# Mix-out in two pairs of column blocks, with earlier loads of the memory's and the residual's rows

## The chip, the cores and the metric

The kernel runs on one core of one Trainium2 chip. The metric is the device time of one execution in microseconds (us). Engines: PE (TensorE) multiplies, PEld is its weight load, DVE (VectorE) and ACT (ScalarE) do elementwise work, POOL (GpSimd) a few small operations, SP (SyncE) issues the DMAs. SBUF is the on-chip memory, PSUM the accumulator that PE writes.

## The reference

One decoder layer over 256 tokens of width 2048, all in fp32. In outline:

```python
hn = rmsnorm(h, norm_mix_w)
q, k, v, g_ret, xr, yr, g_a, g_b = split(hn @ w_in)
ret_out = silu(g_ret) * head_groupnorm(retention(q, k, v))
rnn_out = gelu(yr) * rg_lru(causal_conv(xr))
merged = sigmoid(g_a) * (ret_out @ w_proj_ret) + sigmoid(g_b) * (rnn_out @ w_proj_rnn)
h = h + merged @ w_mix_out                       # "mix-out"
h = h + memory_cross_attention(rmsnorm(h), rmsnorm(mem), xa_w_q, xa_w_k, xa_w_v, xa_w_o)
h = h + conv_gated_ffn(rmsnorm(h))
out = rmsnorm(h, final_norm_w)
```

`mem` is 256 fixed memory tokens of width 2048. The change lies between `w_proj_ret` and the first product of the cross-attention, `mem_n @ xa_w_k`.

## The kernel before

Each fp32 operand is split into a high and a low part in the fp32r type, and a product of two operands is three matmuls (high x high, low x high, high x low). Tokens are two tiles of 128 (`tt`), the sum runs over k-tiles of 128 (16 of them for width 2048), and the output columns come in blocks of 512 (`BW`). A matmul here is always 128x128 weights against 512 columns.

Weights are streamed once from one array in the order of use (`weight_plan`, `weight_stream`). `prefetch` loads a chunk of 1 MB into one of three buffers called `raw`; `weight_parts` makes the high part with an ACT cast (`hi`, L351) and the low part with a DVE subtraction (`lo`, L352), into six buffers of each. It runs two chunks ahead of PE (`AHEAD`).

A product with a weight comes in two forms. `steps_n` does one block of 512 columns; a chunk is four k-tiles. `steps_pair` does two blocks together; a chunk is two k-tiles (a "k-pair") of both blocks. Both chunks are 24 matmuls. In a pair, chosen k-pairs (the tuple `seven`) are done in seven block products in place of eight: the two token tiles, the two k-tiles and the two column blocks make a 2x2x2 block product, and sums and differences of blocks are multiplied. That is 21 matmuls. It asks for sums of the weights (`seven_parts`: four DVE additions at L372, and seven half-size parts in place of four) and sums of the left operand (`sums_of`, L450 to L461), kept in a table (`token_sums`) for the next product with the same operand. The result of a pair is put together from its PSUM banks by one ACT copy (L518), four DVE operations (L525) after the last seven-product k-pair, and four more (L536) at its end.

The work of a pair or block is followed by a step that needs it transposed. `by_dma` copies rows into two 16-bit planes (ACT, L558, called planes below), transposes them by a DMA from SP (L559), and some chunks later `join` puts the words together (ACT, L571) and hands them on. `later(n, fn)` runs `fn` when `n + 1` more chunks have been written down. Large tiles share 29 buffers (`big`). A scheduler orders each engine's instructions by their place in the program and by when they could run; the matmuls keep the program's order.

Around the change: the gates `g_a` are two pairs of `w_in` (L999 to L1002), then come two pairs of `w_proj_ret` (L1003 to L1007). Each of their four results is gated, added (L978, L1006) and sent through `by_dma` to `turn_merged`, which makes two left operands of mix-out from each block, eight in all. Then `residual` does mix-out in four single blocks. Its first three blocks are run by halves: the first half of k of blocks 0, 1 and 2, then the second half of each, and then block 3 (`by_halves` puts the weights in that order). Just before it, eight loads of 512 KB are issued: four of the rows of `x` (`hrow`, the residual) and four of the rows of `mem`. During it the squares of `mem` are summed (ACT, L646), the mean is turned into a factor, and the first four transposed and split tiles of `mem` (`ms`) are made (L617 on ACT, L618 on DVE). After each block the residual is added (L1029), the sum goes through `by_dma` to `turn` (split of the next left operand, L617 and L618), and its squares are taken (ACT, L1047). Four rows are parked in HBM. The same `residual` serves `xa_w_o`, with its first two blocks as a pair.

Of the kernel before, what the change touches and what calls it, by code (L numbers as in the profile page):

```python
# [20 lines left out]
NT = D // P  # L21
# [7 lines left out]
BW = 512  # L29
# [14 lines left out]
SEVEN_U = (4,)  # L44
MORE_U = (2, 4)
SEVEN_V = (5,)

O_Q, O_K, O_V, O_G = 0, 1024, 2048, 4096
O_XR, O_YR, O_GA, O_GB = 6144, 8192, 10240, 12288
# [26 lines left out]
def weight_plan():  # L76

    plan = []
    for g in range(2):
        keys = [("w_in", 0, NT, c + g * BW) for c in (O_Q, O_K)]  # L80
        values = [("w_in", 0, NT, O_V + b * BW) for b in range(2)]
        plan += keys + [both("w_in", O_V + 1024, SEVEN_V)] if g else [keys[0], values[0], keys[1], values[1]]
        plan.append(both("w_in", O_G + g * 1024))
    for b in range(4):
        plan += [("w_in", 0, NT, c + b * BW) for c in (O_XR, O_YR)]
    plan += [("w_in", 0, NT, O_GB + b * BW) for b in range(2)] + [both("w_proj_rnn", 0)]
    plan += [both("w_in", O_GB + 1024), both("w_proj_rnn", 1024)]
    plan += [both(w, c + b * BW) for w, c in (("w_in", O_GA), ("w_proj_ret", 0)) for b in (0, 2)]
    plan += [("w_mix_out", 0, NT, b * BW) for b in range(4)]
    plan += [both("xa_w_k", 0, SEVEN_V), both("xa_w_q", 0), both("xa_w_q", 2 * BW), both("xa_w_k", 2 * BW)]  # L90
    plan += [both("xa_w_v", 0)] + [("xa_w_v", 0, NT, b * BW) for b in (2, 3)]
    plan += [both("xa_w_o", 0, SEVEN_O)] + [("xa_w_o", 0, NT, b * BW) for b in (2, 3)]
    for kind, *a in ff_plan():
        if kind == "down" and sum(a) < NF // 4:
            plan += [both("ffn_w_down", b * BW, SEVEN, a[0] * BW, 4 * a[1]) for b in (0, 2)]
        elif kind == "down":
            plan += [("ffn_w_down", a[0] * BW, 4 * a[1], b * BW) for b in range(4)]
        else:
            plan.append(both("ffn_w_up", a[0] * BW, MORE_U if plan[-1][0] != "ffn_w_up" else SEVEN_U, apart=FF))
    return plan  # L100
# [28 lines left out]
    return [c for o in products for c in o[:-1]] + [o[-1] for o in products]  # L129


def by_halves(products):

    return [c for part in (slice(0, 2), slice(2, 4)) for o in products for c in o[part]]


def weight_stream():

    out = [
        [(w, row + k * P, n, (*c[:2], k // KH in c[2]) if isinstance(c, tuple) else c) for k, n in pieces(i, nk, c)]  # L140
        for i, (w, row, nk, c) in enumerate(weight_plan())
    ]
    out[:2] = [[one for pair in zip(*out[:2]) for one in pair]]
    out[-4:-1] = [in_turn(out[-4:-1])]
    i = [c[0][0] for c in out].index("w_mix_out")
    out[i : i + 3] = [by_halves(out[i : i + 3])]
    return [one for chunks in out for one in chunks]


# [17 lines left out]
def hybrid_layer(  # L167
# [47 lines left out]
    def load_rows(src, c, cs=slice(0, BW), t=None):  # L215

        if t is None:
            t = big([P, 2, BW], s="nat")
        rows = src[0].rearrange("(t p) d -> p t d", p=P)
        sp.dma_start(out=t[:, :, cs], in_=rows[:, :, c * BW + cs.start : c * BW + cs.stop])  # L220
        return t
# [34 lines left out]
    plan = weight_plan()  # L256
# [122 lines left out]
    def later(n, fn):  # L379

        pending.append((step[0] + n + 1, fn))
# [156 lines left out]
    def pair(*args):  # L538
        return ended(steps_pair(*args))
# [10 lines left out]
    def by_dma(rows, then, wait=1, pin=False):  # L550


        planes = big([P, 2, 2, BW], U16, s="pl")
        turned_ = big([P, 2, 4, S], U16, s="pt")
        words = rows.bitcast(U16).rearrange("p t (n h) -> p t h n", h=2)
        for tt in range(2):
            with tc.high_priority(FREE):
                act.copy(planes[:, tt], words[:, tt])  # L558
            turning = sp.dma_start_transpose(  # L559
                out=turned_.rearrange("p h f s -> p (h f) s")[:, :, tt * P : (tt + 1) * P],  # L560
                in_=planes[:, tt].rearrange("p h n -> p (h n)"),
            )
            if pin:
                behind.append(turning.ins)

        def join():
            f = big([P, 4, S], s="f")
            halves_ = f.bitcast(U16).rearrange("p f (s h) -> p h f s", h=2)
            for tt in range(2):
                cs = slice(tt * P, (tt + 1) * P)  # L570
# [16 lines left out]
    def split_pair(src, scale=None):  # L587

        t = big([P, 2, BW], F32R, s="s")
        if scale is None:  # L590
            act.copy(t[:, :, 0:S], src)
            dve.tensor_tensor(out=t[:, :, S:BW], in0=src, in1=t[:, :, 0:S].bitcast(F32), op=ALU.subtract)
        else:
            act.mul(t[:, :, 0:S], src, scale)
            dve.scalar_tensor_tensor(
                out=t[:, :, S:BW], in0=src, scalar=scale, in1=t[:, :, 0:S].bitcast(F32),
                op0=ALU.mult, op1=ALU.subtract,
            )
        return t
# [48 lines left out]
    def sums():  # L648
        return sp_.tile([P, 2, 4], F32, tag="ss0", name=nm("ss"))
# [327 lines left out]
    def gated(t, z):  # L977
        dve.scalar_tensor_tensor(out=z, in0=t, scalar=1.0, in1=z, op0=ALU.add, op1=ALU.mult)  # L978

    merged = []  # L980

    def turn_merged(f):
        for pr in range(2):
            merged.append(split_pair(f[:, 2 * pr : 2 * pr + 2, :], 0.5))

    ts, mb = [], []
    for b in range(2):
# [9 lines left out]
            mb.append(z)  # L997
    for h in range(HEADS):
        later(4 + h, lambda h=h: split_head(h))  # L999
    ts = []  # L1000
    for b in (0, 2):
        ts += [tanh_rows(a, a) for a in pair("w_in", 0, xs, NT, O_GA + b * BW, O_GA + (b + 1) * BW)]  # L1002
    for b in (0, 2):  # L1003
        for i, m in enumerate(pair("w_proj_ret", 0, ret, NT, b * BW, (b + 1) * BW)):
            gated(ts[b + i], m)
            dve.tensor_add(m, m, mb[b + i])  # L1006
            by_dma(m, turn_merged, 1 + (b + i == 3))  # L1007


    hrow = [load_rows(x, c) for c in range(4)]  # L1010
    mnat = [load_half(mem, i) for i in range(4)]
    ms = Pairs(mem_t, p_mem, 3)

    def residual(w, st, out, wcol, steps=None):

        ss = sums()
        products = [steps_n(w, 0, st, NT, b * BW) for b in range(4)]
        sources = []
        for b in range(4):
            if steps:  # L1020
                steps(b)
                if b == 0:
                    for one in products[:3]:
                        for _ in range(2):
                            next(one)
            elif b == 0:
                sources += pair(w, 0, st, NT, 0, BW)
            h = hrow[b]
            dve.tensor_add(h, h, sources.pop(0) if sources else ended(products[b]))  # L1029
            by_dma(h, lambda f, b=b: turn(f, b, out, wcol), 1 + (b == 1), b == 3 and steps is None)  # L1030
            if b < 2:
                later(2 + b, lambda h=h, b=b: squares(h, ss, b))
            else:
                squares(h, ss, b)
        return ss

    def turn(f, b, out, wcol):
        for pr in range(2):
            out.append(split_cols(f[:, 2 * pr : 2 * pr + 2, :], lambda j: wcol(4 * b + 2 * pr + j)))
# [6 lines left out]
        junk = tp.tile([P, BW], F32, tag="tmp", name=nm("junk"))  # L1046
        act.activation(junk[:, 0 : y.shape[1]], y, AF.Square, accum_out=o)  # L1047

    rsms = []

    def memory_steps(b):
        if b == 0:
            ss = sums()[:, :, 0:2]
            for c in range(4):
                later(5 + c, lambda c=c: sum_squares(mnat[c], ss, c))
            later(9, lambda: rsms.append(rstd_rows(ss)))
        if b == 2:
            ms.load(2)
            for k2 in range(4):
                later(2 + k2, lambda k2=k2: ms[k2])  # L1060

    h1s, parked = [], []

    def park(h):
# [1 line left out]
        sp.dma_start(out=t, in_=h)  # L1066
        parked.append(t)

    ss1 = residual("w_mix_out", merged, h1s, p_xa, memory_steps)


    for h in hrow:
# [53 lines left out]
    osp = []  # L1126
# [31 lines left out]
        hrow[b] = t  # L1158

    h2s = []  # L1160
    ss2 = residual("xa_w_o", osp, h2s, p_ffn)
    rs2 = rstd_rows(ss2)


# [180 lines left out]
```

## Time and profile before

| | us |
|---|---|
| median of 3 runs | 1983.33 |
| lowest, highest | 1981.59, 1983.79 |
| the profiled execution's own time | 1982.85 |
| its span in the trace | 1980.9 |
| PE busy in the span | 1961.0 |
| DVE busy in the span | 1644.8 |
| ACT busy in the span | 1394.1 |

The profile's page gives the busy time of each engine and lists groups of instructions by line. A view by stretches of time gives the busy time of each engine in each stretch, the granted clock of TensorE, the share of the DMA engines and their rate. A timeline lists instructions in order with their start, their duration, and in brackets the idle time of the engine before them and who ended it. The busy time of PE is modelled: consecutive matmuls overlap in the list, so what a matmul takes is read from the distance between starts. A row "x2" is two matmuls that follow each other.

### The profile page before, as it was taken

The numbers are of one execution on the slowest core, as the hardware profiler recorded it, in microseconds if no ns is written. First come the engines' busy times: TensorE is split into PE (matmuls) and PEld (weight loads), VectorE is DVE, ScalarE is ACT, GpSimd is POOL, SyncE is SP. The second block draws the span as 40 slices with busy tenths as digits, with TensorE's granted clock in tenths as the row PEclk, the third lists the DMA queues.
The fourth block names the chain that finished last, engine by engine and source line by source line (L and its number), as shares of the span: only waits on it lengthen the run. The fifth ranks groups of instructions, "written<-read, shape, count | busy, mean of one in ns | idle before, by whom it ended". The sixth has DMA issues, their size and how long they took to land. (4 is left out here: it accounts for less than half of the span.)

```text
span 1980.9 us, 24128 instructions
## 1 busy us (share of the span) xinstructions
PE 1961.0 (99%) x8798; PEld 1624.5 (82%) x8798; DVE 1644.8 (83%) x2176; ACT 1394.1 (70%) x1714; POOL 31.6 (2%) x25
## 2 busy tenths in 40 slices
PE   9999999999999999999999999999999999999998
PEld 8888888888888888788888888888877888878887
DVE  6887986899898888668888767888889889899786
ACT  6666658989654656697778677787886477774783
POOL 0000001010000000000000000100000000000000
PEclk9999999999999999999999999999999999999999
DMA  8755567665554555897766666577765576665673
GB/s 332 239 213 169 198 245 204 204 223 192 211 211 173 192 212 192 297 308 245 214 222 215 210 216 219 197 230 212 233 203 182 212 232 213 214 201 204 231 252 110
DMA packets 198344, 429.82 MB, mean 217 GB/s; under 512 B 142161, under 2 KB 146769, under 8 KB 153169
## 3 DMA queue, kind: packets, MB, share of 16 engines
q1 hardware_dynamic: 198224, 428.28, 64.5%
q8 instruction: 69, 1.13, 0.2%
q14 instruction: 51, 0.41, 0.1%
HBM read 390.49 MB, written 4.19 MB: 199 GB/s over the span
## 5 line engine op out<-in xcount | busy, mean ns | idle before, releaser
L352 DVE TENSOR_TENSOR lo<-raw,hi 128x1024 fp32r<-128x1024 f32 (+1 forms) x818 | 953.7, 1189 | 249.2 <-ACT hi L351 244.0
L253 PE MATMUL acc<-hi,s 128*128 128x512 f32 (+1 forms) x3632 | 1113.9, 388 | 0.9 <-ACT hi L351 0.8
L351 ACT CAST hi<-raw 128x1024 fp32r<-128x1024 f32 (+1 forms) x818 | 807.8, 1018 | 417.2 <-DMA raw<-in_wall 111.3
L253 PEld LDWEIGHTS acc<-hi,s 128*128 128x128 f32 x3632 | 679.3, 188 | 140.2 <-ACT hi L351 1.5
L253 PE MATMUL acc<-lo,s 128*128 128x512 f32 (+1 forms) x1816 | 704.5, 388 | 3.9 <-DVE lo L352 3.8
L253 PE MATMUL sm<-hi,s 128*128 128x512 f32 x1568 | 482.9, 389 | 0.0
L253 PEld LDWEIGHTS acc<-lo,s 128*128 128x128 f32 x1816 | 341.2, 188 | 76.3 <-DVE lo L352 6.5
L253 PEld LDWEIGHTS sm<-hi,s 128*128 128x128 f32 x1568 | 294.4, 188 | 61.1
L253 PE MATMUL sm<-lo,s 128*128 128x512 f32 x784 | 305.5, 390 | 2.8 <-DVE lo L352 2.7
L571 ACT COPY f<-pt 128x1024 uint16<-128x1024 uint16 x128 | 166.3, 1353 | 14.8 <-DMA pt<-pl 14.6
L253 PEld LDWEIGHTS sm<-lo,s 128*128 128x128 f32 x784 | 147.2, 188 | 34.8 <-DVE lo L352 4.5
L372 DVE TENSOR_TENSOR raw<-raw 128x512 f32<-128x512 f32 x208 | 143.1, 688 | 3.7
L253 PE MATMUL acc<-hi,ts 128*128 128x512 f32 x312 | 96.2, 389 | 0.0
L558 ACT COPY pl<-o 128x1024 uint16<-128x1024 uint16 x68 | 66.7, 1039 | 7.9 <-DVE o L1006 5.2
L253 PEld LDWEIGHTS acc<-hi,ts 128*128 128x128 f32 x312 | 58.5, 188 | 12.2 <-ACT hi L351 0.2
L253 PE MATMUL acc<-lo,ts 128*128 128x512 f32 x156 | 61.5, 394 | 1.7 <-DVE lo L352 1.7
L558 ACT COPY pl<-rows 128x1024 uint16<-128x1024 uint16 x40 | 39.8, 1042 | 21.1 <-DVE rows L584 10.9
L525 DVE TENSOR_TENSOR o<-o,acc 128x512 f32<-128x512 f32 x62 | 42.2, 681 | 0.2
L536 DVE TENSOR_TENSOR o<-o,acc 128x512 f32<-128x512 f32 x62 | 39.6, 680 | 2.9 <-PE acc L253 2.7
L536 DVE TENSOR_TENSOR o<-o,sm 128x512 f32<-128x512 f32 x62 | 40.8, 680 | 0.3
L1172 DVE SCALAR_TENSOR_TENSOR fv<-f,pf,fv 128x255 f32<-128x255 f32 (+1 forms) x88 | 38.7, 479 | 1.7 <-ACT fv L1170 1.5
L525 DVE TENSOR_TENSOR o<-acc,o 128x512 f32<-128x512 f32 x62 | 39.7, 682 | 0.3
(191 smaller groups left out, 1062.6 us busy)
## 6 DMA issues: line engine op xcount, KB each, us to landing
raw<-in_wall SPq DMA_DIRECT2D x352, 1024.0 KB, 4.8
nat<-in_x SPq DMA_DIRECT2D x8, 512.0 KB, 9.1
raw<-in_wall SPq DMA_DIRECT2D x7, 512.0 KB, 6.1
pt<-pl SPq DMA_TRANSPOSE x128, 3.3
nat<-in_mem SPq DMA_DIRECT2D x4, 512.0 KB, 8.7
home<-nat SPq DMA_DIRECT2D x4, 512.0 KB, 6.2
nat<-home SPq DMA_DIRECT2D x4, 512.0 KB, 7.3
xt<-in_x_t SPq DMA_DIRECT2D x3, 512.0 KB, 8.5
```

Source lines behind the costliest of these rows:

```text
L253: tc.keep_in_program_order(pe.matmul(*a, **k))
L351: act.copy(hi[:, cs], src[:, cs])
L352: dve.tensor_tensor(out=lo[:, cs], in0=src[:, cs], in1=hi[:, cs].bitcast(F32), op=ALU.subtract)
L372: dve.tensor_tensor(out=o, in0=a, in1=b, op=ALU.add)
L525: dve.tensor_tensor(out=o, in0=a, in1=b, op=op)
L536: dve.tensor_tensor(out=o, in0=o, in1=banks[a], op=ALU.add)
L558: act.copy(planes[:, tt], words[:, tt])
L571: act.copy(halves_[:, :, :, cs], turned_[:, :, :, cs])
L1172: dve.scalar_tensor_tensor(out=y[:, s:S], in0=z[:, j, 0 : S - s], scalar=pf[:, 2 - s, t : t + 1], in1=y[:, s:S], op0=ALU.mult, op1=ALU.add,)
```

## The change

Mix-out becomes two pairs: blocks 0 and 1 with k-pair 2 in seven products, blocks 2 and 3 with k-pairs 2 and 5. The order by halves is gone. The four loads of `mem` are issued one by one during the pairs of `g_a` (7, 9, 11 and 13 chunks after their start), each with its squares two chunks later. The factor of `mem` and the first two loads of its transposed tiles come four chunks into `w_proj_ret`. The four loads of the residual's rows come one per chunk in the second pair of `w_proj_ret` (after 9 to 12 of its two pairs' 16 chunks). The first four tiles `ms` are made from the join of the third block of `merged` on, two chunks apart. The join waits of mix-out's results become 1, 2, 1, 2 chunks (they were 1, 2, 1, 1). `xa_w_o` keeps its form.

```diff
+SEVEN_M = (2,)
-    plan += [("w_mix_out", 0, NT, b * BW) for b in range(4)]
+    plan += [both("w_mix_out", 0, SEVEN_M), both("w_mix_out", 2 * BW)]
-def by_halves(products):
-    return [c for part in (slice(0, 2), slice(2, 4)) for o in products for c in o[part]]
-    i = [c[0][0] for c in out].index("w_mix_out")
-    out[i : i + 3] = [by_halves(out[i : i + 3])]
...
-    merged = []
+    merged, rsms, hrow = [], [], []
+    ms = Pairs(mem_t, p_mem, 3)
+    ss_mem = sums()[:, :, 0:2]
+    def memory_squares(c):
+        t = load_half(mem, c)
+        later(1, lambda: sum_squares(t, ss_mem, c))
+    def memory_begun():
+        rsms.append(rstd_rows(ss_mem))
+        ms.load(2)
     def turn_merged(f):
         for pr in range(2):
             merged.append(split_pair(f[:, 2 * pr : 2 * pr + 2, :], 0.5))
+            if len(merged) == 5:
+                for k2 in range(4):
+                    later(2 + 2 * k2, lambda k2=k2: ms[k2])
...
+    for c in range(4):
+        later(6 + 2 * c, lambda c=c: memory_squares(c))
     ts = []
     for b in (0, 2):
         ts += [tanh_rows(a, a) for a in pair("w_in", 0, xs, NT, O_GA + b * BW, O_GA + (b + 1) * BW)]
+    later(3, memory_begun)
+    for b in range(4):
+        later(8 + b, lambda b=b: hrow.append(load_rows(x, b)))
...
-    hrow = [load_rows(x, c) for c in range(4)]
-    mnat = [load_half(mem, i) for i in range(4)]
-    ms = Pairs(mem_t, p_mem, 3)
-    def residual(w, st, out, wcol, steps=None):
+    def residual(w, st, out, wcol, paired):
...
         for b in range(4):
-            if steps:
-                steps(b)
-                if b == 0:
-                    for one in products[:3]:
-                        for _ in range(2):
-                            next(one)
-            elif b == 0:
-                sources += pair(w, 0, st, NT, 0, BW)
+            if b in paired:
+                sources += pair(w, 0, st, NT, b * BW, (b + 1) * BW)
             h = hrow[b]
             dve.tensor_add(h, h, sources.pop(0) if sources else ended(products[b]))
-            by_dma(h, lambda f, b=b: turn(f, b, out, wcol), 1 + (b == 1), b == 3 and steps is None)
+            by_dma(h, lambda f, b=b: turn(f, b, out, wcol), 1 + (b % 2 if b in (*paired, *(i + 1 for i in paired)) else 0), b == 3 and w == "xa_w_o")
...
-    def memory_steps(b):
-        if b == 0:
-            ss = sums()[:, :, 0:2]
-            for c in range(4):
-                later(5 + c, lambda c=c: sum_squares(mnat[c], ss, c))
-            later(9, lambda: rsms.append(rstd_rows(ss)))
-        if b == 2:
-            ms.load(2)
-            for k2 in range(4):
-                later(2 + k2, lambda k2=k2: ms[k2])
...
-    ss1 = residual("w_mix_out", merged, h1s, p_xa, memory_steps)
+    ss1 = residual("w_mix_out", merged, h1s, p_xa, (0, 2))
...
-    ss2 = residual("xa_w_o", osp, h2s, p_ffn)
+    ss2 = residual("xa_w_o", osp, h2s, p_ffn, (0,))
```

More of the change, by code (lines that the diff above doesn't have):

```diff
@@ L1047, in square @@
         act.activation(junk[:, 0 : y.shape[1]], y, AF.Square, accum_out=o)
-    rsms = []
-    def memory_steps(b):
-        if b == 0:
-            ss = sums()[:, :, 0:2]
-            for c in range(4):
-                later(5 + c, lambda c=c: sum_squares(mnat[c], ss, c))
-            later(9, lambda: rsms.append(rstd_rows(ss)))
-        if b == 2:
-            ms.load(2)
-            for k2 in range(4):
-                later(2 + k2, lambda k2=k2: ms[k2])
     h1s, parked = [], []
```

## The prediction

> **What bounds the kernel now.** I read the page first, then a table of busy time by stretches, then the order of time on PE, ACT, DVE and SP around mix-out.
>
> ```profile
> span 1980.9 us, 24128 instructions
> PE 1961.0 (99%) x8798; PEld 1624.5 (82%) x8798; DVE 1644.8 (83%) x2176; ACT 1394.1 (70%) x1714; POOL 31.6 (2%) x25
> ```
>
> PE bounds the kernel: it is idle for 20 us of the span. Only fewer matmuls or fewer PE waits can make it faster; work on the others counts where it makes PE wait. In the stretches the columns are PE, PEld, DVE, ACT and POOL busy, then clock, DMA share and GB/s:
>
> ```profile
> 678.00:720.00 42.00, 42.00 (x187) 34.80 (x186) 40.44 (x56) 27.66 (x37) 0.00 (x0) 1.00 0.59 214
> 763.00:805.00 42.00, 41.73 (x184) 34.27 (x183) 36.05 (x42) 29.42 (x32) 0.00 (x0) 1.00 0.58 190
> 780.00:800.00 20.00, 19.73 (x87) 16.04 (x86) 17.87 (x23) 14.49 (x17) 0.00 (x0) 1.00 0.54 202
> 805.00:894.00 89.00, 87.63 (x385) 71.94 (x385) 57.08 (x68) 70.73 (x96) 0.70 (x1) 1.00 0.91 297
> 820.00:840.00 20.00, 18.63 (x82) 14.80 (x80) 6.28 (x8) 11.22 (x12) 0.00 (x0) 1.00 1.02 367
> 894.00:938.00 44.00, 44.00 (x195) 36.42 (x194) 38.46 (x54) 31.28 (x45) 0.69 (x1) 1.00 0.79 271
> ```
>
> The second pair of `g_a` is the first row, the second pair of `w_proj_ret` the second, mix-out the fourth (805 to 894), the pair of `xa_w_k` the last. Mix-out is the stage where DVE is slack (57 of 89) and the DMA engines are not: at 820 to 840 their share is 1.02 at 367 GB/s, DVE falls to 6.28 of 20, and PE loses time there:
>
> ```profile
> 836.33 0.62 PE L253 MATMUL acc<-hi,s 128*128 128x512 f32 x2
> 837.01 0.62 PE L253 MATMUL acc<-hi,s 128*128 128x512 f32 x2
> 838.69 0.73 PE L253 MATMUL acc<-hi,s 128*128 128x512 f32 x2 [0.84 <-ACT hi L351]
> 840.29 0.63 PE L253 MATMUL acc<-hi,s 128*128 128x512 f32 x2
> 821.01 2.11 SPq L220 DMA_DIRECT2D nat<-in_x  x4
> 823.16 2.39 SPq L224 DMA_DIRECT2D nat<-in_mem  x4
> 825.65 20.69 SPq L224 DMA_DIRECT2D raw<-in_wall  x6
> 837.60 1.99 ACT L351 CAST hi<-raw 128x1024 fp32r<-128x1024 f32 x2 [7.12 <-DMA raw<-in_wall]
> ```
>
> Three matmuls take 837.01 - 836.33 = 0.68 us, so one takes 0.2267. Without a wait the group at 838.69 would start at 837.69 and the one at 840.29 at 838.37: 1.92 us are lost. SP issues the eight loads, then the weights, and the cast that ends the wait is 12 us behind that first weight load. No other PE wait lies in mix-out.
>
> **The change, part by part.** *Matmuls.* Three k-pairs go from 24 to 21 matmuls: 9 x 0.2267 = 2.04 us gone from PE, which nothing hides. The Trainium skill ("TensorE: Matmul & The Clock Gate", section "Wait — 56ns, not 53.3ns?") gives 215.7 ns from start to start for warm matmuls of 512 columns; by that it would be 1.94 us, and the whole forecast 0.1 us later. The trace disagrees with it (226.7 ns at clock 1.00) and decides.
>
> *The eight loads* leave the place in front of the weights. SP would issue the next weights at about 821.0 and the DMA engines would have 4 MB less in front of them, so the 1.92 us go. They come back at 5.4 us apart or wider, where the engines have room: 4 x 0.52 MB over 20 us add 105 GB/s to the 202 of 780 to 800, 307 against the 367 seen above. Bound of the cost there: nothing, or the whole 1.92 again; I take nothing, as 860 to 880 bore 303 GB/s without a wait of PE. SP's time for them (2.11 and 2.39 us) moves too, spread over eight chunks.
>
> ```profile
> 860.00:880.00 20.00, 20.00 (x90) 16.53 (x89) 13.24 (x19) 20.00 (x34) 0.70 (x1) 1.00 0.96 303
> L646 ACT ACTIVATE nat<-nat 128x1024 f32<-128x1024 f32 x4 | 4.2, 1050 | 0.0
> ```
>
> *The squares of mem* (1.05 us each on ACT) move from mix-out into the pairs of `g_a`, where ACT works 27.66 of 42; I cost them at nothing. DVE is the cover's weak side (40.44 of 42): if one square holds up a cast, up to 1.05 us shows. By the code the large tiles then in use are 8 + 2 of the normed input, 4 + 4 results, 8 + 2 of `ret`, 28, and a tile of `mem` makes 29 of 29; the squares must free it in time. The later `mem` factor and first tiles are hidden as they are now.
>
> *DVE's new work* is the main unknown. Seven products cost these rows more:
>
> ```profile
> 768.01 2.87 DVE L372 TENSOR_TENSOR raw<-raw 128x512 f32<-128x512 f32 x4
> 773.00 4.63 DVE L352 TENSOR_TENSOR lo<-raw,hi 128x1024 fp32r<-128x1024 f32 x4 [2.12 <-ACT hi L351]
> 940.94 0.69 DVE L450 TENSOR_TENSOR g<-s 128x512 f32<-128x512 f32 x1
> 946.18 0.69 DVE L461 TENSOR_TENSOR ts<-tq,ts 128x512 fp32r<-128x512 f32 x1
> L525 DVE TENSOR_TENSOR o<-o,acc 128x512 f32<-128x512 f32 x62 | 42.2, 681 | 0.2
> L1029 DVE TENSOR_TENSOR nat<-nat,acc 128x1024 f32<-128x1024 f32 x3 | 3.7, 1217 | 0.5 <-PE acc L253 0.5
> ```
>
> Per seven-product k-pair, four additions (2.87) and 1.5 more splits of 4.63 / 4 = 1.16: 4.6 us, 13.8 for three. Sums of two left operands: the two rows of 0.69 and about 1 us of small ones between, 4.8 together. Putting two pairs together: 16 operations of 0.68, 10.9. That is 29.5 us on top of 57.1, less 1.7 as one join more falls behind mix-out: 85 in 375 x 0.2267 = 85.0 us. Back-to-back operations overlap by 0.06 to 0.1 us, which takes some 2 us off. DVE goes from 64% to about 98%, and `xa_w_k` behind it stands at 38.46 of 44 already and gets some 3 us more. The pair of `g_a` shows that 96% over 42 us goes without a wait; over 129 us there is no row. So I look where a seven-product k-pair may come late.
>
> First pair, k-pair 2: PE reaches it 10.9 us after 805.05, at 815.9. DVE must first finish 4.6 us of gating (until 811.3), as it did in front of the pair at 763, whose k-pair 2 was in time. New is the sum of the left operand, which PE needs as its second product, 0.9 us in. In front of the pair of `xa_w_q`, which begins at 938, the last row of that sum (946.18) ended at 946.9, 8.9 us in, without gating; with gating 4.6 later, 13.5 against 11.8 needed, 1.7 late. The 2.12 us that DVE idles at 773 could hold 1.7 of it. Between 0 and 1.7 I take 0.9.
>
> Second pair, k-pair 5: the nearest rows are those of the second pair of `xa_w_q`, which has the same planes, joins and k-pairs:
>
> ```profile
> 981.16 3.89 ACT L558 COPY pl<-o 128x1024 uint16<-128x1024 uint16 x4 [1.52 <-DVE o L536]
> 997.78 1.14 ACT L591 CAST s<-f 128x512 fp32r<-128x512 f32 x2
> 998.82 0.61 ACT L351 CAST hi<-raw 128x512 fp32r<-128x512 f32 x1
> 1003.63 7.02 DVE L352 TENSOR_TENSOR lo<-raw,hi 128x1024 fp32r<-128x1024 f32 x6
> 1006.24 0.62 PE L253 MATMUL sm<-hi,ts 128*128 128x512 f32 x2
> 863.16 1.98 ACT L558 COPY pl<-nat 128x1024 uint16<-128x1024 uint16 x2
> 873.44 1.70 ACT L617 ACTIVATE s<-f,pb 128x256 fp32r<-128x256 f32 x4
> 865.04 0.63 ACT L1047 ACTIVATE junk<-nat 128x512 f32<-128x512 f32 x1
> ```
>
> ACT is full there from 981.16 to 999.4. The split that ends at about 1004.8 is needed two products behind 1006.24, at 1007.6: 2.8 us to spare. In mix-out's second pair the planes start 1.2 us later (first residual addition), and before the same casts ACT has 1.1 us more for the two joins (1.70 against 1.14), one block's squares (1.6), two `ms` tiles (1.8) and the cast of a sum (0.6): 6.3 - 2.8 = 3.5 us late. If squares and `ms`, not needed soon, give way, 0.1. The row nearest to it is that of `w_proj_ret`, where joins and k-pair 5 met:
>
> ```profile
> 790.88 0.61 PE L253 MATMUL acc<-hi,ts 128*128 128x512 f32 x2
> 792.11 0.63 PE L253 MATMUL acc<-hi,ts 128*128 128x512 f32 x2
> ```
>
> Those starts are 1.23 apart in place of 0.68, 0.55 lost. Between 0.1 and 3.5 I take 1.2.
>
> `xa_w_k`, k-pair 5: planes, join and squares of one more block (1.98 + 4.3 + 1.6 us of ACT) fall in front of it; ACT idled 7.6 us between 894 and 920. Between 0 and 2 I take 0.4.
>
> *Sum* against the profiled execution (1982.85, 1.95 over its span, 0.48 below the median): -2.04 - 1.92 + 0.9 + 1.2 + 0.4 = -1.46. Against the median of 1983.33 that is 1981.9. About 0.2%, 4 us, is what a measurement of this kernel can tell from no change.
>
> **The rivals.**
> *A, all is kept.* The scheduler fills DVE's and ACT's gaps, as at 678 to 720, and no k-pair is late: 1983.33 - 3.96 = 1979.4. For it: DVE idles 2.12 us just before a cast at 773; against it: ACT has no such gap from 981 to 999.
> *B, the wait at 838 is not the loads'.* SP also spent 815.8 to 821.0 on two transposes, and these stay. Then only the matmuls go, and the new waits come: 1983.33 - 2.04 + 2.5 = 1983.8. Against it: the weights issued at 825.65 landed only for 837.60, while the page's median for them is 4.8 us.
>
> ```profile
> raw<-in_wall SPq DMA_DIRECT2D x352, 1024.0 KB, 4.8
> 1506.32 0.63 PE L253 MATMUL acc<-hi,s 128*128 128x512 f32 x2
> 1508.60 0.49 PE L253 MATMUL acc<-lo,s 128*128 128x512 f32 x1 [1.65 <-DVE lo L352]
> 1508.93 0.63 PE L253 MATMUL acc<-hi,s 128*128 128x512 f32 x2
> ```
>
> *C, DVE becomes the bound* from mix-out's first k-pair 2 to the end of `xa_w_k`, and the time ends slower. Where DVE is full today, at 1505 in the feed-forward part, PE's starts of 1506.32 and 1508.93 are 2.61 apart, not 0.68: 1.93 lost at each such place. Four seven-product k-pairs, each late in its additions and again in its second half, are eight places, 15.4 us; without slack between, some 5 of 8 would show, 9.7 us: 1983.33 - 3.96 + 9.7 = 1989.1. It decides the sign where DVE's lateness passes 3.96 us, and shows above 0.2% from 7.9. For it: 98% of DVE over 85 us; against it: three chunks of split weights (16 us of PE) stand between.
>
> **How the numbers follow.** My forecast 0.42 (1979.6 to 1985.5 with the bounds above), A 0.24, B 0.10, C 0.24. A's time stands at 0.2% itself; three quarters of it, 0.18, count as faster with what luck elsewhere gives. Forecast, B and the rest of A lie within 0.2%: 0.58. Slower: C, 0.24. Predicted is the forecast, 1981.9. The range takes in A with half a us of scatter, 1978.9, and reaches C at 1989.1, leaving its longer half out.
>
> **What would show it.** 9 matmuls fewer; no wait on `raw` in front of PE near 838, and no DMA share near 1 there; DVE above 90% from 805 to 890. Right if PE's waits between 805 and 935 are on `lo` or `ts` at the seven-product k-pairs and total 1 to 5 us. Wrong if they exceed 8, if PE waits between 660 and 805 where it did not, or if the loads find no free tile.

## The result and the profile after

The changed kernel takes 1995.26 us (median of 4 runs, 1993.65 to 2000.62) against 1983.18 for the kernel before: a ratio of 1.0067, with a 95% interval of 1.0054 to 1.0080. (A ratio here is worked out over all the runs, so it is not quite that of the medians.) It is slower by 12 us, where 1981.9 was forecast with a range up to 1989.1.

From the page of the changed kernel, whose lines moved by some numbers (L253 became L247, L351 L345, L352 L346, L372 L366, L450 L444, L460 L454, L461 L455, L525 L519, L536 L530, L558 L552, L571 L565, L617 and L618 L611 and L612, the gating's last addition L1006 became L1019, the residual's L1029 L1032; in a run that adds a line at the top of the file each is one further):

```profile
span 1993.5 us, 24161 instructions
PE 1964.7 (99%) x8789; PEld 1625.3 (82%) x8789; DVE 1672.7 (84%) x2220; ACT 1401.3 (70%) x1724; POOL 32.3 (2%) x25
```

There are nine matmuls fewer (8798 to 8789), and PE is busy 3.7 us longer. Those two do not fit together unless matmuls became slower. The table by stretches shows where (columns as before):

```profile
800.00:820.00 20.00, 16.55 (x73) 13.30 (x71) 19.96 (x26) 12.14 (x14) 0.00 (x0) 0.96 0.72 207
820.00:840.00 20.00, 19.95 (x77) 16.00 (x77) 16.90 (x21) 16.43 (x21) 0.00 (x0) 0.87 0.74 276
850.00:894.00 44.00, 42.65 (x183) 33.77 (x182) 37.74 (x53) 33.88 (x48) 0.00 (x0) 1.00 0.64 204
920.00:940.00 20.00, 13.62 (x50) 10.14 (x49) 17.36 (x29) 14.31 (x22) 0.00 (x0) 0.83 0.42 156
```

At 820 to 840 PE is busy all the time with 77 matmuls where 88 fit, at a granted clock of 0.87; at 920 to 940 it does 50, at 0.83. The DMA share at 820 to 840 is 0.74 where it was 1.02. The waits are these, in order of time on PE; the first four rows belong to the first pair's k-pair 2, the last three to `xa_w_k`'s k-pair 5:

```profile
815.74 0.39 PE L247 MATMUL acc<-lo,s 128*128 128x512 f32 x1
819.58 1.64 PE L247 MATMUL sm<-hi,ts 128*128 128x512 f32 x2 [3.45 <-ACT ts L454]
821.44 1.05 PE L247 MATMUL acc<-hi,s 128*128 128x512 f32 x2
822.72 1.05 PE L247 MATMUL acc<-hi,ts 128*128 128x512 f32 x2
...
927.37 0.50 PE L247 MATMUL acc<-hi,s 128*128 128x512 f32 x1 [0.95 <-DVE s L612]
933.53 1.52 PE L247 MATMUL sm<-hi,ts 128*128 128x512 f32 x2 [5.43 <-ACT ts L454]
935.28 1.05 PE L247 MATMUL acc<-hi,s 128*128 128x512 f32 x2
```

`ts` is the sum of the left operand that a seven-product k-pair needs as its second product. Behind each wait three matmuls take 822.72 - 821.44 = 1.28 us, 0.427 each, where 0.227 is usual. The Trainium skill ("TensorE: Matmul & The Clock Gate", section "What's actually happening") says that TensorE's clock falls to half after an idle window of about 3.4 us and comes back after a busy one, and its section "Wait — 56ns, not 53.3ns?" gives 426.7 ns for such a matmul. The trace agrees on the 0.427. It agrees on the half clock too (the granted clock is 0.50 from 818.42 to 825.25 and from 931.06 to 937.89) but not on the length of the idle time: the clock fell 2.3 us after PE's last matmul had ended at 816.13.

I count as lost each distance between starts beyond 0.2267 us per matmul, where it is more than 0.1 us:

| us lost by PE in | before | after |
|---|---|---|
| second pair of `w_proj_ret` | 0.55 | 0.55 |
| mix-out's first half or pair | 1.92 | 6.58 |
| mix-out's second half or pair | 0 | 2.74 |
| pair of `xa_w_k` | 0 | 9.09 |
| the rest of the attention | 1.57 | 0.49 |

That is 15.4 us more; less 2.04 for the matmuls it is 13.4, and the span grew by 12.6; the 0.8 us between them lie in distances that the table leaves out. So the gain came (the wait at 838 is gone, nine matmuls too), and the two places with a long wait on `ts` cost 15.7 us (6.58 and 9.09). Such losses are given for the runs below too.

### The profile page after: what moved, and what is told of

The parts are those of the page before. It is cut to its first block, busy times and chain, and to the rows that moved or that the text cites. A ratio compares the mean times of both kernels' runs of the same rounds, so it can differ in the third digit from the quotient of the medians.

```text
span 1993.5 us, 24161 instructions
## 1 busy us (share of the span) xinstructions
PE 1964.7 (99%) x8789; PEld 1625.3 (82%) x8789; DVE 1672.7 (84%) x2220; ACT 1401.3 (70%) x1724; POOL 32.3 (2%) x25
## 4 chain that ended last, share of the span: by engine, by line
PE 50%; DVE 4%; ACT 2%; DMA 1%; issue 1%; POOL 0%; POOLq 0%; DVEq 0%; ACTq 0%
PE acc L247 31%; PE sm L247 19%; DVE lo L346 2%; DMA raw<-in_wall 1%; ACT f L565 1%; ACT hi L345 0%; DMA pt<-pl 0%; DVE fv L1162 0%; ACT pl L552 0%; DVE o L519 0%; DVE raw L366 0%; DVE s L612 0%; DVE fg L1162 0%; DVE s L589 0%; ACT junk L1050 0%
## 5 line engine op out<-in xcount | busy, mean ns | idle before, releaser
L346 DVE TENSOR_TENSOR lo<-raw,hi 128x1024 fp32r<-128x1024 f32 (+1 forms) x824 | 963.2, 1191 | 238.7 <-ACT hi L345 230.8
L345 ACT CAST hi<-raw 128x1024 fp32r<-128x1024 f32 (+1 forms) x824 | 813.5, 1017 | 411.8 <-PE sm L247 109.5
L247 PE MATMUL acc<-hi,s 128*128 128x512 f32 (+1 forms) x3498 | 1073.1, 388 | 1.0 <-DVE s L612 0.9
L247 PEld LDWEIGHTS acc<-hi,s 128*128 128x128 f32 x3498 | 654.7, 188 | 135.1 <-DVE s L612 1.6
L247 PE MATMUL acc<-lo,s 128*128 128x512 f32 (+1 forms) x1749 | 678.4, 388 | 3.4 <-DVE lo L346 3.3
L247 PE MATMUL sm<-hi,s 128*128 128x512 f32 x1672 | 515.0, 389 | 0.0
L247 PEld LDWEIGHTS acc<-lo,s 128*128 128x128 f32 x1749 | 328.7, 188 | 72.5 <-DVE lo L346 4.6
L247 PEld LDWEIGHTS sm<-hi,s 128*128 128x128 f32 x1672 | 313.7, 188 | 65.2 <-DVE o L530 0.3
L247 PE MATMUL sm<-lo,s 128*128 128x512 f32 x836 | 325.7, 390 | 3.3 <-DVE lo L346 3.2
L247 PEld LDWEIGHTS sm<-lo,s 128*128 128x128 f32 x836 | 156.9, 188 | 37.6 <-DVE lo L346 5.0
L565 ACT COPY f<-pt 128x1024 uint16<-128x1024 uint16 x128 | 166.0, 1354 | 14.9 <-DMA pt<-pl 14.8
L366 DVE TENSOR_TENSOR raw<-raw 128x512 f32<-128x512 f32 x220 | 151.6, 689 | 3.9
L247 PE MATMUL acc<-hi,ts 128*128 128x512 f32 x330 | 103.4, 395 | 0.2
L552 ACT COPY pl<-o 128x1024 uint16<-128x1024 uint16 x68 | 66.7, 1040 | 13.3 <-DVE o L1019 11.0
L247 PEld LDWEIGHTS acc<-hi,ts 128*128 128x128 f32 x330 | 62.9, 191 | 14.6 <-ACT hi L345 1.5
L247 PE MATMUL acc<-lo,ts 128*128 128x512 f32 x165 | 65.8, 399 | 2.9 <-DVE lo L346 2.9
L552 ACT COPY pl<-rows 128x1024 uint16<-128x1024 uint16 x40 | 39.8, 1042 | 21.4 <-DVE rows L578 11.3
L519 DVE TENSOR_TENSOR o<-o,acc 128x512 f32<-128x512 f32 x66 | 44.9, 681 | 0.5 <-ACT o L512 0.3
L530 DVE TENSOR_TENSOR o<-o,acc 128x512 f32<-128x512 f32 x66 | 42.2, 681 | 3.2 <-PE acc L247 3.0
L247 PE MATMUL sm<-hi,ts 128*128 128x512 f32 x110 | 35.9, 405 | 8.9 <-ACT ts L454 8.9
L530 DVE TENSOR_TENSOR o<-o,sm 128x512 f32<-128x512 f32 x66 | 43.7, 682 | 0.5 <-PE sm L247 0.2
L519 DVE TENSOR_TENSOR o<-acc,o 128x512 f32<-128x512 f32 x66 | 42.4, 683 | 0.3
```

The source lines that it names most:

```text
L247: tc.keep_in_program_order(pe.matmul(*a, **k))
L345: act.copy(hi[:, cs], src[:, cs])
L346: dve.tensor_tensor(out=lo[:, cs], in0=src[:, cs], in1=hi[:, cs].bitcast(F32), op=ALU.subtract)
L366: dve.tensor_tensor(out=o, in0=a, in1=b, op=ALU.add)
L519: dve.tensor_tensor(out=o, in0=a, in1=b, op=op)
L530: dve.tensor_tensor(out=o, in0=o, in1=banks[a], op=ALU.add)
```

## The experiments

Two theories fit these rows. *Late sum*: each of the two long waits is one left operand's sum that stands too late in the order of DVE and ACT; with the sum earlier, it goes, and nothing comes in its place. *Saturation* (the forecast's rival C): DVE has too much work from 805 to 940, and PE waits for something in any order. Both leave open how much of the loss is the clock.

**The first sum early.** (In the cuts of code, `...` stands for lines left out.)

```diff
         for pr in range(2):
             merged.append(split_pair(f[:, 2 * pr : 2 * pr + 2, :], 0.5))
+            if len(merged) == 3:
+                sums_of(merged[2])
```

> The sum of merged's third tile (the left operand of the first pair's seven products) is made as soon as that tile exists, some 20 us before mix-out, instead of during mix-out's first chunk; nothing else is changed. Late-sum theory: the wait of 3.45 us on ts in the first pair and the slow matmuls behind it go, 6.6 us in all; the DVE work moves into the second pair of w_proj_ret, whose k-pair 5 may wait up to 2 us more. Time 1988.5 to 1991. Saturation theory (DVE simply has too much work from 805 on): the 2.4 us of DVE work taken out of that stretch are all that is gained; the wait moves from ts to lo. Time about 1993 to 1994.5.

1990.56 us (1.0041, 1.0025 to 1.0057). The first pair loses nothing (6.58 before this edit), the second pair of `w_proj_ret` 2.07 (0.55), `xa_w_k` still 10.1. The stretch of the first pair, in the table by stretches:

```profile
805.00:850.00 45.00, 45.00 (x200) 37.24 (x200) 41.21 (x48) 31.40 (x37) 0.00 (x0) 1.00 0.77 267
```

PE is full at clock 1.00 with DVE 92% busy. That speaks against saturation: DVE did more there than in the changed kernel (36.7 of 45), and PE did not wait.

**The memory's tile and sum early.**

```diff
-                for k2 in range(4):
+                for k2 in range(6):
                     later(2 + 2 * k2, lambda k2=k2: ms[k2])
+                later(13, lambda: sums_of(ms[5]))
```

> Two more tiles of the transposed memory (the fifth and sixth) are made during mix-out's second pair, and the sum of the sixth, the left operand of xa_w_k's seven products, one chunk before xa_w_k; nothing else is changed. Late-sum theory: the waits of 0.95 and 5.43 us in xa_w_k and the slow matmuls behind them go, 9.2 us in all, less what 4 us more DVE work in the second pair cost there. Time 1986 to 1989. Saturation theory: the same work in a stretch that is as full; the wait moves into the second pair or to lo in xa_w_k. Time 1993 to 1996.

1987.20 us (1.0024, 1.0010 to 1.0038). `xa_w_k` loses nothing; the first pair, which the edit does not touch, still loses 5.79, the second 2.58.

```profile
894.00:940.00 46.00, 46.00 (x205) 38.07 (x204) 43.01 (x60) 36.47 (x52) 1.60 (x1) 1.00 0.82 276
```

DVE is at 43.01 of 46 (93%), and PE has no gap. At both places the wait went when the sum came earlier, without less work. That nothing comes in its place holds for `xa_w_k` alone: the first edit cost 1.5 us in front of mix-out.

**The waits filled with idle work.** A loop in front of the second product of the last seven-product k-pair multiplies into a bank that its first product overwrites later.

```diff
+FILL = {("w_mix_out", 0): 15, ("xa_w_k", 0): 26}
...
+                    if name == "x3" and k2 == last:
+                        for _ in range(FILL.get((w, c1), 0)):
+                            mm(banks["p6"], own[0][0][0], parts[0][0], start=True, stop=False, skip_group_check=True)
```

> PE gets idle work for the two long waits: 15 matmuls into a bank that the next product overwrites anyway, between the first and the second product of the first pair's seven products, and 26 at the same place in xa_w_k. They fill 3.4 and 5.9 us in which PE stood still, and change nothing else. Clock theory (the wait itself throttles TensorE, and the matmuls behind it take 0.427 us instead of 0.227): clock 1.00 throughout, the matmuls behind both waits at 0.227, 4.5 us saved, about 1990.5. Late-operand theory (the matmuls behind the waits are slow because their operands trickle in): no change, about 1995.

1990.69 us (1.0041, 1.0026 to 1.0056), 4.6 us less than the changed kernel with 41 matmuls more. The first place on PE:

```profile
816.15 3.56 PE L248 MATMUL acc<-hi,s 128*128 128x512 f32 x15
819.77 0.50 PE L248 MATMUL sm<-hi,ts 128*128 128x512 f32 x1
820.60 0.50 PE L248 MATMUL sm<-hi,ts 128*128 128x512 f32 x1 [0.33 <-DVE ts L456]
821.17 0.62 PE L248 MATMUL acc<-hi,s 128*128 128x512 f32 x2
```

`ts` comes as late as ever (819.77 against 819.58), but the matmuls behind it stay at 0.227. The first place loses 0.94 and 15 x 0.2267 = 3.40 of idle work, 4.34 in place of 6.58; the second 1.08 + 5.89 = 6.97 in place of 9.09. So the clock is 2.2 and 2.1 us of the two losses, shown by taking it away (in this run it is 1.00 at both places); the rest is waiting.

**The seven products one k-pair later.**

```diff
-SEVEN_M = (2,)
+SEVEN_M = (3,)
+SEVEN_N = (3, 5)
...
-    plan += [both("w_mix_out", 0, SEVEN_M), both("w_mix_out", 2 * BW)]
+    plan += [both("w_mix_out", 0, SEVEN_M), both("w_mix_out", 2 * BW, SEVEN_N)]
```

> The seven products of the first pair stand at k-pair 3 instead of 2, those of the second pair at 3 and 5 instead of 2 and 5 (so the sum is still made once). As much work everywhere, but the sum and the weights' additions are needed 5.4 us later. Late-sum theory: the first wait goes, as its sum was 3.5 us late; about 6.6 us saved, 1988.5 to 1990. Saturation theory: as much work in as much time, PE waits as long at the next place; 1993 to 1996.

1991.72 us (1.0050, 1.0033 to 1.0067); above the late-sum range by more than a us, below that of saturation. The profiled execution was the fastest of four, at 1986.22. In it the first pair loses 2.55, not nothing: the waits on `ts` are 1.42 and 0.58 us, without a slower clock. 5.4 us more of time took only 2 us off the lateness of 3.45. In the code both kernels write the sum down in the pair's first chunk, but on DVE it now starts at 817.97, behind the four additions for k-pair 3, where it started at 813.73 between those for k-pair 2; why the scheduler moved it back, no run shows. The second pair loses 0.33 (2.74); that the earlier seven-product k-pair lies at 3 may be why, but this was not tested by itself.

**The loads alone.** The kernel before, mix-out in single blocks by halves, with the loads, the memory's squares, its factor and the first two loads of its transposed tiles where the change has them (the two functions are the change's).

```diff
+    for c in range(4):
+        later(6 + 2 * c, lambda c=c: memory_squares(c))
...
+    later(3, memory_begun)
+    for b in range(4):
+        later(8 + b, lambda b=b: hrow.append(load_rows(x, b)))
...
-    hrow = [load_rows(x, c) for c in range(4)]
-    mnat = [load_half(mem, i) for i in range(4)]
...
```

> The kernel before with one part of the change: the loads and squares of the memory's rows and the loads of the residual's rows stand where the change puts them; mix-out stays in four single blocks by halves. If the eight loads in front of the weights made the wait at 838 us, its 1.92 us go and nothing comes in their place: 1981.2, no wait of PE in mix-out. If the transposes on SP made it, the wait stays: 1983. If the loads now hold up the weights of the products before mix-out, a wait on raw appears between 690 and 805 and the time is above 1983.

1979.03 us: 0.9982 of before, 0.9973 to 0.9991. Faster by 3.6 us, and faster than both kernels. Its stretch at the old wait:

```profile
820.00:840.00 20.00, 20.00 (x90) 16.57 (x89) 12.03 (x12) 12.04 (x13) 0.00 (x0) 1.00 0.85 287
```

PE is full, DVE works 12.03 where it had 6.28, and the DMA share is 0.85. The trace shows 1.92 us less lost in mix-out and 1.5 less behind the attention, which the edit does not touch; where the second comes from stays open.

**The pairs alone.** The eight loads back in front of mix-out, with the memory's squares in its first pair.

```diff
-        later(1, lambda: sum_squares(t, ss_mem, c))
+        later(5 + c, lambda: sum_squares(t, ss_mem, c))
...
-    for c in range(4):
-        later(6 + 2 * c, lambda c=c: memory_squares(c))
...
-    later(3, memory_begun)
-    for b in range(4):
-        later(8 + b, lambda b=b: hrow.append(load_rows(x, b)))
...
+    hrow += [load_rows(x, c) for c in range(4)]
+    for c in range(4):
+        memory_squares(c)
+    ms.load(2)
+    later(9, lambda: rsms.append(rstd_rows(ss_mem)))
```

> The change without its moved loads: mix-out in two pairs with three k-pairs in seven products, the eight loads in front of mix-out and the memory's squares during its first pair, as before. Late-sum theory: the waits on ts in the first pair and in xa_w_k stay (about 6.6 and 9 us), and the 1.92 us that the moved loads are worth come back unless the first wait covers them: 1994.5 to 1997.5. If the moved loads and squares had a part in the two waits, it is clearly below 1993.

2003.69 us (1.0096, 1.0079 to 1.0112), above every expectation. The loss is 9.82, 6.84 and 9.13 in the first pair, the second and `xa_w_k`. Its first wait, on DVE and PE:

```profile
816.00 4.63 DVE L346 TENSOR_TENSOR lo<-raw,hi 128x1024 fp32r<-128x1024 f32 x4 [0.40 <-ACT hi L345]
820.55 0.68 DVE L444 TENSOR_TENSOR g<-s 128x512 f32<-128x512 f32 x1
823.05 1.52 PE L247 MATMUL sm<-hi,ts 128*128 128x512 f32 x2 [6.58 <-ACT ts L454]
```

Here the whole sum stands behind four splits, of which the last two belong to the next chunk. DVE is busy with work that PE needs 5 us later, while PE waits 6.58 us for work whose operand has long been there. The order alone makes this wait. That the moved loads and squares were worth more than 1.92 us beside the pairs is measured (2003.69 against 1995.26); how the order comes to differ between the two kernels is not explained by the runs.

**The joins later, the factor later.** Two edits on what stands in front of the tile and the sum of `xa_w_k`. The first puts the joins of mix-out's third and fourth block 3 and 4 chunks later:

```diff
-by_dma(h, ..., 1 + (b % 2 if b in (*paired, *(i + 1 for i in paired)) else 0), ...)
+by_dma(h, ..., 2 * b if w == "w_mix_out" and b > 1 else 1 + (b % 2 if b in (*paired, *(i + 1 for i in paired)) else 0), ...)
```

> The joins of mix-out's third and fourth block are put 3 chunks later (waits 4 and 6 instead of 1 and 2), so that their 8.5 us of ACT and 3.3 us of DVE fall behind the tile and the sum that xa_w_k's seven products need; no work is added or taken away. ACT theory (in xa_w_k the tile of the memory and its sum are late because two blocks' planes, squares and joins stand in front of them on ACT, where it was one block before): the waits of 0.95 and 5.43 us shrink below 2 us together and the clock stays at 1.00 there, 6 to 9 us saved, 1986 to 1989. If DVE's total work decides, less than 2 us is saved.

The second delays the reduction of the squares:

```diff
-    dve.tensor_scalar_mul(lscale, rstd_rows(ss1), float(XD**-0.5))
+    later(5, lambda: dve.tensor_scalar_mul(lscale, rstd_rows(ss1), float(XD**-0.5)))
```

> The reduction of the residual's squares and the factor made from it come 6 chunks later, so that DVE no longer stands 3.02 us for ACT's squares and 0.81 us for POOL at the start of xa_w_k (906 to 911 us). If that standing makes the tile and the sum late, the wait of 5.43 us on ts shrinks by about 3.8 us, falls below what throttles the clock, and 5 to 6 us are saved: 1989 to 1990.5. If ACT's order decides, DVE waits for ACT's casts instead and less than 1.5 us is saved.

With the joins later `xa_w_k` loses nothing (9.09), at clock 1.00; 3.1 us come back in the next pair, `xa_w_q`, which now waits 2.00 and 0.58 us for its own sum, and the time is 1992.12 (1.0040, 1.0026 to 1.0053), above the range that was expected. Its profiled execution, the slowest of five at 1995.76, also lost 6 us more behind the attention than the changed kernel's, at places where the code is the same; that stays open. With the factor later nothing is won, 1995.32 (1.0061, 1.0046 to 1.0077), but the edit hardly tested its theory: the scheduler left the reduction where it was, and DVE still stands 3.01 us there. The rows of the changed kernel for this place, ACT first:

```profile
903.12 3.89 ACT L552 COPY pl<-nat 128x1024 uint16<-128x1024 uint16 x4 [0.31 <-DVE nat L1032]
910.32 2.57 ACT L565 COPY f<-pt 128x1024 uint16<-128x1024 uint16 x2
919.23 2.56 ACT L565 COPY f<-pt 128x1024 uint16<-128x1024 uint16 x2
924.73 0.90 ACT L611 ACTIVATE s<-xt,pb 128x256 fp32r<-128x256 f32 x2
926.84 0.87 DVE L612 SCALAR_TENSOR_TENSOR s<-xt,pb,s 128x256 fp32r<-128x256 f32 x2
928.35 3.49 DVE L346 TENSOR_TENSOR lo<-raw,hi 128x1024 fp32r<-128x1024 f32 x3
931.76 0.42 DVE L450 TENSOR_TENSOR tq<-g 128x256 f32<-128x256 f32 x1
```

Planes of two blocks at once, two joins, then the tile of the memory at 924.73 to 927.7. PE has reached the k-pair at 926.03; the sum begins only at 927.75, is cut by three splits (3.49 us) and ends at 934.2. With the joins later the sum's first operation is at 916.0 instead of 927.8. So the joins in front made the tile late, as ACT's theory says; the edit moved 3.3 us of DVE work along with them, so ACT's share alone is not separated. That the splits then cut the sum is a second part of the same wait.

**Both sums early.** The first two edits together.

```diff
+            if len(merged) == 3:
+                sums_of(merged[2])
...
-                for k2 in range(4):
+                for k2 in range(6):
...
+                later(13, lambda: sums_of(ms[5]))
```

> The change with both sums early: merged's third tile is summed as soon as it exists (as in the run with that alone), and the memory's fifth and sixth tile and the sum of the sixth are made in mix-out's second pair. Late-sum theory: both long waits go (6.6 and 8.9 us); 1.5 us more in the second pair of w_proj_ret and 2.5 us in mix-out's second pair stay, against 2.04 for the matmuls and 1.92 for the loads: 1982.8, the same as before within 1.5 us, and slower than the loads alone (1979.0). Saturation theory: the work taken out of both places shows as waits elsewhere between 763 and 940, above 1986.

1984.71 us (1.0006, 0.9996 to 1.0016): not to be told from before, 0.4 us beyond what late sum allowed and below saturation's. Mix-out's first pair and `xa_w_k` lose nothing, the second pair 2.56, and the second pair of `w_proj_ret` 6.06 in the profiled execution: there ACT waited 2.36 us for the weights of its k-pair 5 (0.17 in the changed kernel), the early sum stood in the same place, and the clock fell. The run with the first sum alone had lost 2.07 at the same place with the same code.

**Both sums early, k-pair 3.** The edits for k-pair 3 and for the memory's tile, and a sum that comes two chunks after its tile.

```diff
+SEVEN_M = (3,)
+SEVEN_N = (3, 5)
...
+            if len(merged) == 4:
+                later(1, lambda: sums_of(merged[3]))
```

> As the run with both sums early, but the first pair's seven products stand at k-pair 3 and the second's at 3 and 5, and the sum of merged's fourth tile is made two chunks after that tile, behind the additions of w_proj_ret's last seven products. Late-sum theory: no wait on ts; the second pair of w_proj_ret loses the 0.55 us of before, mix-out's pairs together under 1.5 us, xa_w_k nothing: matmuls and loads are kept, 1977 to 1980, as fast as the loads alone or up to 2 us faster. Saturation theory: 4 us or more of waits on lo appear in mix-out, above 1982.

1979.76 us: 0.9990 of before, 0.9981 to 1.0000. The loss in the table's first four places is 1.99 (0.55 was expected), 0, 1.23 and 0; the rest is as late sum had it. DVE works 40.1 of 44, 40.0 of 44 and 41.0 of 44 us from 806 to 938, so 92% for 132 us, and PE loses 1.2 us there. As fast as the loads alone, not faster: what the nine matmuls save is given back in front of mix-out and in its second pair.

**K-pair 4, with three and with two k-pairs in seven products.** The memory's tile and sum are early in both; the second run leaves `SEVEN_N` and the sum of `merged[2]` out and uses `SEVEN_M` for both pairs.

```diff
+SEVEN_M = (4,)
+SEVEN_N = (2, 4)
...
+            if len(merged) == 8:
+                later(2, lambda: sums_of(merged[2]))
```

> Three k-pairs in seven products again, at k-pair 4 of the first pair and 2 and 4 of the second; the sum of merged's third tile is made during the first pair, that of the fifth when its k-pair is near, and the memory's fifth and sixth tile with the sum of the sixth early. Nothing new stands before mix-out. Late-sum theory: the second pair of w_proj_ret loses 0.55 us as before, mix-out under 1.5 us, xa_w_k nothing: 2.04 and 1.92 us are kept, 1977 to 1980. Saturation theory: as much DVE work as the change in as much time, so 4 us or more of waits between 805 and 940; above 1983.

> As the run at k-pair 4, but the second pair has k-pair 4 alone in seven products (two k-pairs in all, 1.36 us of matmuls saved, and 4.6 + 2.4 us less of DVE work). Late-sum theory: no waits worth a us, 1978 to 1980.5, the same as the run with three. Saturation theory: clearly faster than the run with three, as 7 us of DVE work are gone from a full stretch.

1986.01 (1.0014, 1.0005 to 1.0024) and 1983.88 us (1.0007, 0.9998 to 1.0016); both outside what late sum expected. Both wait on the first pair's sum, since nothing makes it early: 0.75 and 0.85 us in the one, 0.75 and 0.84 in the other. And yet the matmuls behind them slow down in the one and not in the other. The run with three:

```profile
828.93 0.50 PE L248 MATMUL sm<-hi,ts 128*128 128x512 f32 x1 [0.75 <-ACT ts L455]
830.28 0.51 PE L248 MATMUL sm<-hi,ts 128*128 128x512 f32 x1 [0.85 <-DVE ts L456]
830.86 0.62 PE L248 MATMUL acc<-hi,s 128*128 128x512 f32 x2
831.56 1.05 PE L248 MATMUL acc<-hi,ts 128*128 128x512 f32 x2
832.84 1.05 PE L248 MATMUL acc<-hi,ts 128*128 128x512 f32 x2
```

From 831.56 on the matmuls take 0.427 for some 3.4 us; in the run with two they stay at 0.227 behind the same waits, and the first pair loses 2.15 in place of 3.73. But the run with two slows down elsewhere: in its profiled execution, the slowest of 11 at 1986.52, ACT waited 1.99 us for the weights of k-pair 5 in the second pair of `w_proj_ret`, where its code is the changed kernel's, the clock is 0.50 from 795.55 to 798.97, and 3.81 us are lost (0.55). Saturation would have the run with fewer sevens clearly faster. It was not, though the intervals of the two overlap and the losses in front of mix-out blur the comparison.

## Why the prediction was wrong, point by point

*Matmuls, -2.04*: right, nine fewer. *The loads, -1.92*: right. The wait at 838 is gone in the changed kernel and in the run of the loads alone, which gained 3.6 us, the 1.92 and some more outside mix-out. Rival B fell with it. That the loads cost nothing where they went held in the profile of the change; in two of the later profiles, both sums early and k-pair 4 with two, ACT waited 2.4 and 2.0 us for weights at that place.

*First pair, k-pair 2, +0.9, bounded by 1.7*: 6.58 measured; by the run with idle work 4.3 of it is waiting and 2.2 the clock. This is the step that failed first. I put the end of the sum 13.5 us into the pair at the latest. Part of that was a misreading. I took it from the pair of `xa_w_q` and let that pair begin at 938; it begins 51 matmuls before 948.44, at 936.9. The second row below is its second product at k-pair 2: the next matmul, at 948.67, needs the sum's last operation, which ended at 946.87, 1.8 us early. With 4.6 us of gating that is 2.8 late, where I had 1.7. The other part is the order of DVE. Two rows of the kernel before, then those of the changed kernel:

```profile
942.44 0.29 DVE L458 TENSOR_TENSOR tq<-g,tq 128x128 f32<-128x128 f32 x1
948.44 0.62 PE L253 MATMUL sm<-hi,ts 128*128 128x512 f32 x2
...
808.39 2.35 DVE L1019 TENSOR_TENSOR o<-o,o 128x1024 f32<-128x1024 f32 x2
813.73 0.69 DVE L444 TENSOR_TENSOR g<-s 128x512 f32<-128x512 f32 x1
814.93 0.42 DVE L450 TENSOR_TENSOR tq<-g 128x256 f32<-128x256 f32 x1
817.00 0.28 DVE L451 TENSOR_TENSOR tq<-tq,g 128x128 f32<-128x128 f32 x1
818.34 0.28 DVE L452 TENSOR_TENSOR tq<-g,tq 128x128 f32<-128x128 f32 x1
818.91 0.61 ACT L454 CAST ts<-tq 128x512 fp32r<-128x512 f32 x1
819.68 0.68 DVE L455 TENSOR_TENSOR ts<-tq,ts 128x512 fp32r<-128x512 f32 x1
```

The gating ends at 810.7 as I had it, and the sum begins 3 us later. Its first four operations, 1.7 us of work, are interleaved one by one with the weights' additions and splits, each of 0.7 or 1.2 us, and take 4.9 us, from 813.73 to 818.62; the same four stood together in `xa_w_q`, from 940.94 to 942.73. With the fifth the sum ends at 820.36, 16.0 us into the pair, 4.2 later than needed; PE had needed the cast at about 816. My shift by 4.6 us moved the sum of `xa_w_q` as a block, and here a block it is not.

*`xa_w_k`, +0.4, bounded by 2*: 9.09 measured, 7.0 of it waiting. Here I let 7.9 us of new ACT work vanish in 7.6 us of idle time. But the rows from 903.12 to 924.73 show ACT taking planes, joins and tile one after the other, and the tile and its sum, which PE needs, were made only when their chunk came near, behind the joins. Idle time earlier in the stretch was no use to them: with the joins behind, the loss is nothing.

*Second pair, k-pair 5, +1.2*: 2.74 measured for the whole pair, inside its bounds of 0.1 to 3.5; two waits on `lo`, 0.53 and 0.71, at k-pair 5 as forecast. Which of the ACT work that I had listed made them was not tested.

*The clock* had no term. The waits set it off, and 2.2 and 2.1 us of the two losses are its share. The rows of before showed a clock of 1.00 beside its wait of 1.92 us, and I didn't ask what a longer one would do; the bounds that I gave the new waits, too short, kept the question away.

*Rival C* named the side, and the stretch, but not the mechanism. It held DVE to be full, 85 of 85 us. DVE works 35.7 of 44 and 37.7 of 44 there in the changed kernel, and up to 93% without a wait of PE where the sums are early. The added work itself was counted well: by the two pages DVE is busy 27.9 us longer in all (1672.7 against 1644.8), where I had 29.5 less 2. C's time of 1989.1 was 6 us short.

*The bounds* of the three waits add up to 1979.5 and 1986.6, not to the 1979.6 and 1985.5 that I wrote; the measured time lies beyond either.

## What to carry to other kernels

In this kernel DVE and ACT were late by what stood in front of the one operation that PE needed next, not by their total work: look up where that operation stands in the order and make it when its operand is ready, before counting busy shares. A bound for a new wait must be taken from the order of instructions after the change, with small operations interleaved, not from the same work as a block elsewhere. Read the row that you shift against the operation that needs it, and not against a round number for the start of its stage. And price a wait of PE with its clock: here 2.1 and 2.2 us came on top of waits of 7.0 and 4.3.

## What the runs showed of the hardware

Short waits can cost the clock: the two waits of 0.75 and 0.85 us in the run at k-pair 4 slowed the matmuls from 831.56 on, and the same two waits in its sister run did not; before, 0.84 and 0.53 did not either. The Trainium skill ("TensorE: Matmul & The Clock Gate", section "HAM oscillation — how this bites in real kernels") puts the rule as no idle gaps above about 3.4 us; these runs show the slower clock behind two gaps of 0.9 and 1.1 us, counted from start to start. Its section "What's actually happening" calls the window free-running. The traces agree, and that settles why equal waits end differently. In all 14 traces the granted clock changes 50 times after its first rise, each time at a whole multiple of 3.413 us from that rise. From 1.00 it fell behind every such step in which PE was busy for less than 47% (by the profile, whose ends of matmuls are modelled), and behind none with more than 54%; between the two both occurred. The first two rows are of the run with three seven-product k-pairs, the last two of the run with two:

```profile
828.11:831.52 3.41, 1.81 (x7) 1.24 (x7) 1.83 (x2) 3.41 (x5) 0.00 (x0) 1.00 0.52 173
831.52:834.93 3.41, 3.41 (x9) 2.64 (x8) 2.67 (x4) 2.69 (x4) 0.00 (x0) 0.50 0.92 382
829.69:833.10 3.41, 2.66 (x13) 1.89 (x11) 2.61 (x5) 1.77 (x3) 0.00 (x0) 1.00 0.92 356
833.10:836.51 3.41, 2.57 (x11) 1.84 (x12) 1.37 (x3) 3.41 (x4) 0.00 (x0) 1.00 0.53 168
```

In the run with three both waits fall into one step, PE is busy for 1.81 of 3.41 us, and the clock of the next step is 0.50. In the run with two the border of a step lies between them, at 833.10, PE is busy for 2.66 and 2.57, and the clock stays at 1.00. So in these traces the clock follows how much of a step PE works, and not the length of one gap.

Whether the moved loads are free differs between executions. Of the 12 profiles with the loads moved, two show ACT waiting for the weights of k-pair 5 in the second pair of `w_proj_ret`, by 2.36 and 1.99 us, and losses of 6.06 and 3.81 us there; the others show at most 0.22, and the two profiles with the loads in front of mix-out nothing. That the loads make these waits is likely from their place, but no run separates it.
